# Attention scores from float16 halves of queries and keys at their own widths, and a half-width last key tile for the values

## The chip, the cores and the metric

One core of one Trainium2 chip runs the kernel. The metric is the device time of one execution in microseconds, the median over the runs. A core has five engines with an instruction stream each: TensorE (PE) multiplies matrices into PSUM, VectorE (DVE) and ScalarE (ACT) move and transform data, GpSimd (POOL) does element-wise work and SyncE (SP) issues most DMAs. ACT evaluates its functions from tables that an instruction of its own, ACT_TABLE_LOAD, exchanges.

## The reference

One step of a hybrid encoder layer on T = 1024 prompt rows and 32 sample rows of 1024 channels, 16 heads of 64. Both kinds of rows share the weights; the sample rows attend to 512 cached keys.

```python
h = rmsnorm(x, norm_g)
q = rmsnorm(h @ Wq, q_g) / 8;  k = rmsnorm(h @ Wk, k_g)      # per head
logf = log_sigmoid(h @ Wf + b_f);  c = cumsum(logf)
s = q @ k.T + c[query] - c[key], causal                        # float32
o = softmax(s) @ v
u = (h @ Wua) * sigmoid(h @ Wub);  conv = causal depthwise conv of width 31 over u
ya = (o * silu(ga)) @ w_pa;  yb = (silu(layernorm(conv)) * silu(gb)) @ w_pb
out = x + (sigmoid(ma) * ya + sigmoid(mb) * yb) @ w_out
```

k, v, logf and the end of u are outputs too. The gains q_g are about eight times as large as k_g in the inputs used.

## The kernel before

**Stages.** The rows stand as 1056 columns (prompt and sample), cut into three chunks of 352, and every float32 operand of a projection is held as two float16 halves, so that one projection is three float16 matmuls per tile (`pj` at L186, `x_split` at L556 for the input). The trace shows the stages at about these times: 0 to 72 us loading, normalising and splitting x with the first u projection; 72 to 205 the rest of u and the values' projection; 205 to 484 queries and keys, with the convolution's taps on DVE (L377); 484 to 570 the gates ga; 570 to 1042 attention, in which PE is filled with the other gates' projections between the attention blocks; 1042 to 1247 the last gates and the projections pa and pb; 1247 to the end the output projection.

**Queries and keys.** `qk` (L889) squares the projection's result, sums the squares of each head by matmuls with a block of ones (`sqh` on ACT, `sql` on POOL at L904, `pst` at L884 and L885), scales to `qn`, and splits `qn` into a high half `qh` (ACT, L929) and a low half `ql` (POOL, L930), both float32r (a float32 whose matmul PE does in one pass). They are written to DRAM as `s_q` and `s_k`. For keys, `qn` also goes out as an output (`kT`, L935) and its sample columns are copied to `ks_t` (L936). `forget_rows` (L846) makes the cumulative sums c of 16 heads on DVE and writes c as two float32r parts with rows of ones to `s_aq` and `s_ak`.

**Attention.** `Head.load` reads a head's halves back as four tiles: QB and KB of 128 rows (low and high halves crossed), QA and KA of 68 rows (high halves and the four rows of c). For each of 8 blocks of 128 queries, `scores` (L1139) does two float32r matmuls per up to 512 keys into `psS`: 128 keys more for each block, in one piece up to 512 and in two equal pieces above, and with at least 256 columns in each (`wm`). `top` subtracts the row's maximum (DVE), `soft` takes the exponential (ACT, L1166), `norm` divides (POOL, L1172), and `turn` transposes the probabilities on PE into `ptr` (L1186), from where ACT copies the first four tiles and DVE the others to `pt` (L1189). Once block 7 is turned, `values` (L1205) does 20 float32 matmuls of 256 query columns, key tile by key tile, on two halves of the array's columns in turn (even tiles j on one, odd ones on the other), into two `po` buffers, which ACT and DVE add into `ot`. For two blocks of queries that share a matmul, the last key tile reaches only the second one; the first one's half of `pt` is set to zero by POOL (L1179). `ptr`, `po` and some sums share one pool of two PSUM buffers, `psT`.

**Order.** Up to attention the order on PE, DVE and ACT is the program's; in attention PE, SP, DVE and ACT keep the program's order; POOL's order there, and after attention all but PE's, is set by a scheduler from the kernel's priorities and dependences. Between attention blocks, `layernorm` (L1239) puts in its pieces one at a time: of these, six pairs of Ln and Exp on ACT over 176 columns each (L1259, L1260) stand among the blocks of heads 8 to 10. After attention `mk_pa` (L1397) loads `sma` and takes a Tanh of it for each tile (L1401).

Of the kernel before, what the change touches and what calls it, by code (L numbers as in the profile page):

```python
# [29 lines left out]
CW = T + 30 + TS  # L30
LNO = ((0,), (1, 2), (3,), (4, 5), (6,), (7,), ())
# [22 lines left out]
def build(tc, xT, xt, wv, wf, ckT, cv, clT, stT, vec, cst, yT, kT, vO, lfO, cpT, csT):  # L54
# [8 lines left out]
    s_q = dram.tile([2, D, T], F32, name="s_q")  # L63
    s_k = dram.tile([2, D, T], F32, name="s_k")
    s_v = dram.tile([8, 128, D], F32, name="s_v")
    s_vs = dram.tile([TS, D], F32, name="s_vs")
    s_aq = dram.tile([H, 4, T], F32, name="s_aq")
    s_ak = dram.tile([H, 4, T], F32, name="s_ak")
# [15 lines left out]
    def f32(ap):  # L84
        return ap.bitcast(F32)
# [366 lines left out]
    with tc.high_priority(offset=9000):  # L452
# [15 lines left out]
        tops = xip.tile([128, 4], F32, name="tops0")  # L468
# [30 lines left out]
    qg8 = cp.tile([128, 1], F32, name="qg8")  # L499
    qs_t = cp.tile([128, 8, TS], F32, name="qs_t")  # L500
# [150 lines left out]

    def consts():
# [3 lines left out]
        nc.vector.tensor_scalar(qg8, vec_t[:, V_QG:V_QG + 1], 0.125, None, op0=ALU.mult)  # L656
# [6 lines left out]
    for f in range(8):  # L663
# [16 lines left out]
        1: [lambda: squares(3)],  # L680
        2: [lambda: low_pool(0, 2, True)],
# [4 lines left out]
        {2: [lambda: behind[0].pop(0)(), lambda: total(2), lambda: known(1)]})  # L686
# [159 lines left out]
    def forget_rows(lfT):  # L846
        on16 = fp.tile([H, T], F32R, name="on16")
        nc.gpsimd.memset(f32(on16), 1.0)
        ls = fp.tile([H, SKEYS], F32, name="ls")
        nc.sync.dma_start(ls[:, :PAST], clT)  # L850
        cc = fp.tile([H, T], F32, name="cc")
        csm = fp.tile([H, SKEYS], F32, name="csm")
        ch, cl, nch, ncl = [fp.tile([H, T], F32R, name=n) for n in ("ch", "cl", "nch", "ncl")]
        V = nc.vector
        ops = [
            (1.4, lambda: V.tensor_tensor_scan(cc, f32(on16), lfT[:, :T], 0.0, op0=ALU.mult, op1=ALU.add)),
            (0.1, lambda: V.tensor_copy(ls[:, PAST:], lfT[:, T:])),
            (0.8, lambda: (V.tensor_tensor_scan(csm, f32(on16)[:, :SKEYS], ls, 0.0, op0=ALU.mult, op1=ALU.add),
                           nc.sync.dma_start(s_cs, csm))),
            (0.8, lambda: V.tensor_copy(ch, cc)),  # L860
            (0.8, lambda: V.tensor_sub(cl, cc, f32(ch))),
            (0.8, lambda: V.tensor_scalar(nch, f32(ch), -1.0, None, op0=ALU.mult)),
            (0.8, lambda: V.tensor_scalar(ncl, f32(cl), -1.0, None, op0=ALU.mult)),
        ]

        def out():
            for dst, rows in ((s_aq, (on16, on16, ch, cl)), (s_ak, (nch, ncl, on16, on16))):
                for i, rw in enumerate(rows):
                    nc.sync.dma_start(dst[:, i, :], f32(rw))
# [19 lines left out]
    def qk(g, f):  # L889
        gv, dst, smp = (vec_t[:, V_KG:V_KG + 1], s_k, ks_t) if g == "k" else (qg8, s_q, qs_t)  # L890
# [33 lines left out]
        def out(c):  # L924
            n = CH if c < 2 else T - 2 * CH
            o = slice(c * CH, c * CH + n)
            qh = tp.tile([128, CH], F32R, name="qh", tag="qh")
            ql = tp.tile([128, CH], F32R, name="ql", tag="ql")
            nc.scalar.copy(qh[:, :n], qn[:, o])  # L929
            nc.gpsimd.tensor_sub(ql[:, :n], qn[:, o], f32(qh[:, :n]))  # L930
            nc.sync.dma_start(dst[0, f * 128:(f + 1) * 128, o], f32(qh[:, :n]))
            nc.sync.dma_start(dst[1, f * 128:(f + 1) * 128, o], f32(ql[:, :n]))
# [40 lines left out]
    class Head:  # L973
# [4 lines left out]
        def load(self):  # L978
            h = self.h
            self.q = [hp.tile([n, T], F32R, name=a, tag=a) for a, n in (("QA", 68), ("QB", 128), ("KA", 68),  # L980
# [3 lines left out]
            nc.sync.dma_start(f32(QB[0:64]), s_q[1, hs, :])  # L984
            nc.sync.dma_start(f32(QB[64:128]), s_q[0, hs, :])
            nc.sync.dma_start(f32(KB[0:64]), s_k[0, hs, :])
            nc.sync.dma_start(f32(KB[64:128]), s_k[1, hs, :])
            nc.sync.dma_start(f32(QA[0:64]), s_q[0, hs, :])
            nc.sync.dma_start(f32(QA[64:68]), s_aq[h])
            nc.sync.dma_start(f32(KA[0:64]), s_k[0, hs, :])  # L990
            nc.sync.dma_start(f32(KA[64:68]), s_ak[h])
# [141 lines left out]
    class Block:  # L1133
# [5 lines left out]
        def scores(self):  # L1139
# [7 lines left out]
            wm = max(w, 256)  # L1147
            for b in range(nb):
                ksl = slice(b * w, b * w + wm)
                nc.tensor.matmul(ps[:, b, :wm], QB[:, qsl], KB[:, ksl], start=True, stop=False)  # L1150
                nc.tensor.matmul(ps[:, b, :wm], QA[:, qsl], KA[:, ksl], start=False, stop=True)  # L1151
# [39 lines left out]
        def values(self):  # L1191
# [9 lines left out]
            for c in range(4):  # L1201
                po = pos[c // 2][:, 256 * (c % 2):256 * (c % 2) + 256]
                for j in range(2 * c + 2):
                    rows = slice(64 * (j % 2), 64 * (j % 2) + 64)
                    nc.tensor.matmul(po[rows], V[:, j, :], parts[c][:, j, :], start=(c % 2 == 0 and j < 2),  # L1205
# [500 lines left out]
```

## Time and profile before

| | |
|---|---|
| median of 3 runs | 1327.76 us (1327.39 to 1329.06) |
| span of the profiled execution | 1331.8 us |
| attention, 570 to 1042 | 472 us |
| DVE busy, whole span | 986.0 us |
| ACT busy, whole span | 693.1 us |
| POOL busy, whole span | 565.2 us |

The profiled execution is taken by the hardware profiler, and its span is 4.0 us above the median of the runs. Start and length of an instruction are in microseconds in the timeline, and nanoseconds stand as "mean ns" in the groups. A matmul's length is its latency: successive matmuls overlap, so what one costs PE is read from the distance of successive starts. LDWEIGHTS loads an operand into the array and overlaps with the matmul before. A wait in brackets says how long the engine sat idle and for what it waited.

### The profile page before, as it was taken

How to read it: one execution, taken by the hardware profiler on the slowest of the kernel's cores; microseconds unless marked ns; L12 is line 12 of the kernel's file. 1: busy time of each engine (PE TensorE's matmuls, PEld its weight loads, DVE VectorE, ACT ScalarE, POOL GpSimd, SP SyncE). 2: the span in 40 equal slices, each digit the busy share in tenths (PEclk: the TensorE clock that was granted, in tenths of full speed). 3: DMA queues.
4: the chain of work that ended last, by engine and by line, in shares of the span. 5: the costliest groups of instructions: out<-in, count | busy, mean ns of one | idle time of the engine just before them, and what ended most of it. 6: DMA issues, size and time to landing. Idle time of an engine off the chain costs nothing.

```text
span 1331.8 us, 24835 instructions
## 1 busy us (share of the span) xinstructions
PE 1311.1 (98%) x9396; PEld 1004.7 (75%) x9396; DVE 986.0 (74%) x1513; ACT 693.1 (52%) x1336; POOL 565.2 (42%) x597
## 2 busy tenths in 40 slices
PE   8999999999999999999899999999999999999999
PEld 5687876666666666677577767767777699999998
DVE  6797879889999998897787875754555388176664
ACT  5644545767686843455545555555555466233320
POOL 4001014637475730245445544342443258255562
PEclk8999999999999999999999999999999999999999
DMA  6243243425252553526545654465561788434461
GB/s 253 99 137 109 86 121 112 146 63 198 86 187 65 186 156 130 164 69 165 147 119 142 181 142 121 114 187 134 150 170 39 247 320 275 157 130 143 126 214 67
DMA packets 113495, 194.96 MB, mean 146 GB/s; under 512 B 34080, under 2 KB 80032, under 8 KB 113376
## 3 DMA queue, kind: packets, MB, share of 16 engines
q1 hardware_dynamic: 113232, 193.31, 46.9%
q8 instruction: 74, 1.21, 0.4%
q14 instruction: 45, 0.37, 0.1%
q10 hardware_dynamic: 144, 0.07, 0.0%
HBM read 127.68 MB, written 65.64 MB: 145 GB/s over the span
## 4 chain that ended last, share of the span: by engine, by line
PE 88%; DVE 7%; ACT 2%; issue 1%; DMA 1%; SPq 1%; POOL 0%; DVEq 0%; ACTq 0%; POOLq 0%
PE pj L186 59%; PE pjv L785 6%; PE pj L1537 6%; PE po L1205 5%; PE ptr L1186 4%; PE psS L1151 2%; PE psS L1150 2%; DVE y L377 2%; DVE wl L144 1%; DVE nm L1159 1%; DMA s_y<-y 1%; PE pst L884 1%; PE pst L885 0%; DMA ga<-s_ga 0%; PE ptx L586 0%
## 5 line engine op out<-in xcount | busy, mean ns | idle before, releaser
L186 PE MATMUL pj<-xl,wh 128*128 128x352 f16 (+2 forms) x1536 | 481.7, 314 | 1.8 <-DVE xl L593 1.6
L186 PE MATMUL pj<-xh,wh 128*128 128x352 f16 (+2 forms) x1536 | 482.2, 314 | 0.8 <-DVE qn L919 0.6
L186 PE MATMUL pj<-xh,wl 128*128 128x352 f16 (+2 forms) x1536 | 481.7, 314 | 0.0
L186 PEld LDWEIGHTS <-wh 128*128 128x128 f16 x3072 | 301.6, 98 | 161.7 <-issue 8.1
L377 DVE SCALAR_TENSOR_TENSOR y<-u,vec_t,y 128x1086 f32<-128x1086 f32 x240 | 348.5, 1453 | 12.1 <-ACT y L374 9.0
L1172 POOL TENSOR_SCALAR P<-P,nm 128x128 f32<-128x128 f32 (+7 forms) x128 | 140.9, 1101 | 203.3 <-DVE nm L1171 181.9
L186 PEld LDWEIGHTS <-wl 128*128 128x128 f16 x1536 | 150.8, 98 | 71.0 <-issue 1.4
L1166 ACT ACTIVATE P<-psS,nm 128x128 f32<-128x128 f32 (+7 forms) x128 | 95.1, 743 | 129.1 <-DVE nm L1171 111.8
L144 DVE SCALAR_TENSOR_TENSOR wl<-raw,sc,wh 128x384 f16<-128x384 f32 x188 | 133.3, 734 | 16.3 <-ACT wh L141 15.8
L1159 DVE TENSOR_REDUCE nm<-psS 128x1 f32<-128x128 f32 (+7 forms) x128 | 97.0, 758 | 10.7 <-POOL P L1172 0.5
L1186 PE MATMUL ptr<-ident,P 128*128 128x128 f32 x576 | 87.2, 274 | 9.8 <-DVE pt L1189 4.7
L1189 ACT COPY pt<-ptr 128x512 f32<-128x512 f32 (+3 forms) x128 | 64.4, 503 | 44.6 <-PE ptr L1186 44.3
L178 POOL TENSOR_TENSOR wl<-raw,wh 128x384 fp32r<-128x384 f32 (+1 forms) x51 | 60.9, 1221 | 61.8 <-ACT wh L175 46.7
L904 POOL TENSOR_TENSOR sql<-sqf,sqh 128x352 fp32r<-128x352 f32 x48 | 57.7, 1203 | 64.9 <-ACT sqh L901 64.9
L1186 PEld LDWEIGHTS ptr<-ident,P 128*128 128x128 f32 x576 | 69.0, 141 | 19.3 <-POOL rstd L357 3.7
L1150 PE MATMUL psS<-KB,QB 128*128 128x256 f32 (+2 forms) x192 | 81.6, 426 | 0.0
L120 POOL CAST topb<-tops 128x2 bf16<-128x2 f32 x35 | 18.6, 532 | 135.9 <-ACT junk L117 86.0
L1205 PE MATMUL po<-pt,V 128*64 128x256 f32 x640 | 72.6, 382 | 2.6 <-ACT pts L1107 2.6
L930 POOL TENSOR_TENSOR ql<-qn,qh 128x352 fp32r<-128x352 f32 (+1 forms) x48 | 67.6, 1424 | 6.1 <-ACT qh L929 6.0
L785 PE MATMUL pjv<-vwh,xh 128*128 128x260 f16 x256 | 70.1, 274 | 0.0
L785 PE MATMUL pjv<-vwl,xh 128*128 128x260 f16 x256 | 70.0, 273 | 0.0
L785 PE MATMUL pjv<-vwh,xl 128*128 128x260 f16 x256 | 69.9, 273 | 0.0
(277 smaller groups left out, 2572.1 us busy)
## 6 DMA issues: line engine op xcount, KB each, us to landing
raw<-wf SPq DMA_DIRECT2D x92, 512.0 KB
QB<-s_q SPq DMA_DIRECT2D x32, 256.0 KB
KB<-s_k SPq DMA_DIRECT2D x32, 256.0 KB
kT<-qn SPq DMA_DIRECT2D x8, 528.0 KB
s_ga<-t SPq DMA_DIRECT2D x24, 176.0 KB
s_gb<-t SPq DMA_DIRECT2D x24, 176.0 KB
s_ma<-t SPq DMA_DIRECT2D x24, 176.0 KB
s_mb<-t SPq DMA_DIRECT2D x24, 176.0 KB
```

The source lines that it names most:

```text
L144: nc.vector.scalar_tensor_tensor(wl[:, ks, :], raw[:, ks, :], self.s[:, i:i + 1], wh[:, ks, :], op0=ALU.mult, op1=ALU.subtract)
L186: nc.tensor.matmul(ps, a[:, kt, :], b(kt, sl), start=(first and n == 0), stop=(last and n == N - 1))
L377: t = nc.vector.scalar_tensor_tensor(y, u[:, i:i + CW], w, y, op0=ALU.mult, op1=ALU.add)
L785: nc.tensor.matmul(ps[:, :VC], a, b, start=(n == 0), stop=(n == 23))
L930: nc.gpsimd.tensor_sub(ql[:, :n], qn[:, o], f32(qh[:, :n]))
L1150: nc.tensor.matmul(ps[:, b, :wm], QB[:, qsl], KB[:, ksl], start=True, stop=False)
L1159: nc.vector.tensor_reduce(nm[:, 0:1], ps[:, :nb, :w], axis=AX.XY, op=ALU.max, negate=True)
L1166: nc.scalar.activation(P[:, :nk].rearrange("p (b w) -> p b w", b=nb), ps[:, :nb, :w], AF.Exp, bias=nm[:, 0:1], accum_out=nm[:, 1:2])
L1172: nc.gpsimd.tensor_scalar(P[:, :nk], P[:, :nk], nm[:, 2:3], 1.0, op0=ALU.mult, op1=ALU.mult)
L1186: nc.tensor.transpose(pt[:, 128 * j:128 * j + 128], P[:, 128 * (4 * u + j):128 * (4 * u + j) + 128], ident)
L1205: nc.tensor.matmul(po[rows], V[:, j, :], parts[c][:, j, :], start=(c % 2 == 0 and j < 2), stop=(c % 2 == 1 and j >= 2 * c))
L1537: nc.tensor.matmul(pss[c][:, :HC], a[:, k, :], x, start=(not more and kt == 0 and n == 0), stop=(kt == 3 and n == 2), skip_group_check=more)
```

## The change

1. Queries, keys and the sums are kept and read as float16: `s_q`, `s_k`, `s_aq`, `s_ak`, `qh`, `ql`, and the tiles QA, QB, KA and KB. The sums c are divided by 64 and written as three float16 parts beside rows of 64, so QA and KA have 70 rows. `forget_rows` has six DVE operations of 16 partitions for the four before.
2. The scores' matmuls have exactly the width of the keys; `wm` is gone, and block 0 has 128 columns.
3. Queries and keys are balanced by a power of two, worked out from the two gains by seven DVE operations of at most two columns and one matmul in the first chunk of `x_split` (`gains`, `balance`). Keys are therefore unscaled again for the output, by a new POOL operation `kun` over 128x1056.
4. In `values`, key tiles alternate between the halves of the array by j + c instead of j, and for c of 1 and more the last tile is multiplied over the second 128 columns alone. The memset of `pt` is left for c = 0.

```diff
-    s_q = dram.tile([2, D, T], F32, name="s_q")
+    s_q = dram.tile([2, D, T], F16, name="s_q")
...
+    def gains():
+        g = vec_t[:, V_QG:V_QG + 2]
+        nc.vector.tensor_mul(tops[:, 4:6], g, g)
+
+    def balance():
+
+        V = nc.vector
+        r = xip.tile([128, 2], F32, name="gr")
+        V.tensor_scalar(bits(r), bits(psq[:, 4:6]), 24, 23, op0=ALU.logical_shift_right, op1=ALU.logical_shift_left)
...
+        V.tensor_scalar(bits(bal[:, 1:2]), bits(r[:, 1:2]), -1.0, float(190 << 23), op0=ALU.mult, op1=ALU.add)
...
-        1: [lambda: squares(3)],
-        2: [lambda: low_pool(0, 2, True)],
+        1: [lambda: squares(3), gains],
+        2: [lambda: low_pool(0, 2, True), balance],
...
-        {2: [lambda: behind[0].pop(0)(), lambda: total(2), lambda: known(1)]})
+        {2: [lambda: behind[0].pop(0)(), lambda: total(2),
+             lambda: nc.tensor.matmul(psq[:, 4:6], ones_w, tops[:, 4:6], start=True, stop=True), lambda: known(1)]})
...
-            (0.8, lambda: V.tensor_copy(ch, cc)),
-            (0.8, lambda: V.tensor_sub(cl, cc, f32(ch))),
-            (0.8, lambda: V.tensor_scalar(nch, f32(ch), -1.0, None, op0=ALU.mult)),
-            (0.8, lambda: V.tensor_scalar(ncl, f32(cl), -1.0, None, op0=ALU.mult)),
+            (0.5, lambda: V.tensor_scalar(rc, cc, 1.0 / CU, None, op0=ALU.mult)),
+            (0.5, lambda: V.tensor_copy(cp3[:, 0, :], rc)),
+            (0.8, lambda: V.tensor_sub(rc, rc, cp3[:, 0, :])),
+            (0.5, lambda: V.tensor_copy(cp3[:, 1, :], rc)),
+            (0.8, lambda: V.tensor_sub(cp3[:, 2, :], rc, cp3[:, 1, :])),
+            (0.8, lambda: V.tensor_scalar(cn3, cp3, -1.0, None, op0=ALU.mult)),
...
             if c == 2:
                 if g == "k":
-                    nc.sync.dma_start(kT[f], qn)
-                nc.gpsimd.tensor_scalar(smp[:, f, :], qn[:, T:TT], 1.0, 1.0, op0=ALU.mult, op1=ALU.mult)
+                    kun = tp.tile([128, TT], F32, name="kun", tag="kun", bufs=1)
+                    nc.gpsimd.tensor_scalar(kun, qn, bal[:, 1:2], 1.0, op0=ALU.mult, op1=ALU.mult)
+                    nc.sync.dma_start(kT[f], kun)
+                    nc.gpsimd.tensor_scalar(smp[:, f, :], kun[:, T:TT], 1.0, 1.0, op0=ALU.mult, op1=ALU.mult)
+                else:
+                    nc.gpsimd.tensor_scalar(smp[:, f, :], qn[:, T:TT], bal[:, 0:1], 1.0, op0=ALU.mult, op1=ALU.mult)
...
-            wm = max(w, 256)
             for b in range(nb):
-                ksl = slice(b * w, b * w + wm)
-                nc.tensor.matmul(ps[:, b, :wm], QB[:, qsl], KB[:, ksl], start=True, stop=False)
-                nc.tensor.matmul(ps[:, b, :wm], QA[:, qsl], KA[:, ksl], start=False, stop=True)
+                ksl = slice(b * w, b * w + w)
+                nc.tensor.matmul(ps[:, b, :w], QB[:, qsl], KB[:, ksl], start=True, stop=False)
+                nc.tensor.matmul(ps[:, b, :w], QA[:, qsl], KA[:, ksl], start=False, stop=True)
...
-                nc.gpsimd.memset(self.head.p[c][:, i + 1, 0:128], 0.0)
+                if c == 0:
+                    nc.gpsimd.memset(self.head.p[c][:, 1, 0:128], 0.0)
...
-                    rows = slice(64 * (j % 2), 64 * (j % 2) + 64)
-                    nc.tensor.matmul(po[rows], V[:, j, :], parts[c][:, j, :], start=(c % 2 == 0 and j < 2),
+                    rows = slice(64 * ((j + c) % 2), 64 * ((j + c) % 2) + 64)
+                    n0 = 128 if c and j == 2 * c + 1 else 0
+                    nc.tensor.matmul(po[rows, n0:], V[:, j, :], parts[c][:, j, n0:], start=(c % 2 == 0 and j < 2),
```

The scheduler also moves work that the diff doesn't name. The first place is ACT's stream in attention, among the blocks of heads 8 to 10, where the layer norm's pairs stand; `t<-pj` empties a gate projection's PSUM, `pt<-ptr` empties the transposes, `P` is the softmax. Before:

```order
L968 ACTIVATE t<-pj,sc 128x352
L1189 COPY pt<-ptr_10056 128x4x128
L1166 ACTIVATE P,nm<-psS,nm 128x384
L117 ACTIVATE junk,tops<-raw 128x1024
L1259 ACTIVATE t<-rstd 128x176
L1260 ACTIVATE t<-t 128x176
L1189 COPY pt<-ptr_10098 128x128
```

The same place now, with the line numbers of the changed kernel (L1289 and L1290 are the pair, L997 the gate's copy, L1218 `pt`, L1194 the softmax):

```order
L997 ACTIVATE t<-pj,sc 128x352
L1289 ACT_TABLE_LOAD
L1289 ACTIVATE t<-rstd 128x176
L1290 ACT_TABLE_LOAD
L1290 ACTIVATE t<-t 128x176
L1218 COPY pt<-ptr_10055 128x4x128
L1194 ACTIVATE P,nm<-psS,nm 128x384
```

Each of the six pairs stands one piece later than before, between a gate's copy and a `pt` copy, and has two table loads, where before it had none. ACT's stream has 26 table loads for 14.

The second place is ACT's stream in attention some heads earlier, around the copies of a head's output `ot`. It reads now:

```order
L1194 ACTIVATE P,nm<-psS,nm 128x640
L1239 COPY ot<-po 64x512
L1431 ACT_TABLE_LOAD
L1431 ACTIVATE sma<-sma 128x352
L1239 COPY ot<-po 64x512
L1431 ACTIVATE sma<-sma 128x352
L1218 COPY pt<-ptr_9088 128x3x128
L1194 ACTIVATE P,nm<-psS,nm 128x768
```

In the kernel before, this table load and the first Tanh of `sma` (there L1401) stand after attention, at the start of pa. Now the first six of the 24 Tanh, and the loads of their tiles on SP, stand within attention, ahead of the six pairs.

The third place is POOL's stream in the queries' and keys' stage, at the end of a key projection. Before:

```order
L904 TENSOR_TENSOR sql<-sqf,sqh 128x352
L896 TENSOR_SCALAR gi<-sc,vec_t 128x1
L936 TENSOR_SCALAR ks_t<-qn 128x32
L904 TENSOR_TENSOR sql<-sqf,sqh 128x352
L930 TENSOR_TENSOR ql<-qn,qh 128x320
```

And now:

```order
L929 TENSOR_TENSOR sql<-sqf,sqh 128x352
L921 TENSOR_SCALAR gi<-sc,kgb 128x1
L961 TENSOR_SCALAR kun<-qn,bal 128x1056
L929 TENSOR_TENSOR sql<-sqf,sqh 128x352
L963 TENSOR_SCALAR ks_t<-kun 128x32
L955 TENSOR_TENSOR ql<-qn,qh 128x320
```

The new `kun` over 1056 columns stands ahead of a `sql`, where a copy of 32 columns stood.

Three smaller moves: head 0's loads of QA, QB, KA, KB and V stand some way earlier on SP; the write of the convolution's `s_y` stands behind later loads instead of ahead of them; DVE has the balance's operations between two `xl` of the first chunk. PE's order is the same, apart from a weight load of its own for each score matmul, the widths, and the one small matmul.

More of the change, by code (lines that the diff above doesn't have):

```diff
@@ L846, in forget_rows @@
     def forget_rows(lfT):
-        on16 = fp.tile([H, T], F32R, name="on16")
-        nc.gpsimd.memset(f32(on16), 1.0)
+        on16 = fp.tile([H, T], F32, name="on16")
+        nc.gpsimd.memset(on16, 1.0)
+        unit = fp.tile([H, T], F16, name="unit")
+        nc.gpsimd.memset(unit, CU)
         ls = fp.tile([H, SKEYS], F32, name="ls")
         nc.sync.dma_start(ls[:, :PAST], clT)
-        cc = fp.tile([H, T], F32, name="cc")
+        cc, rc = [fp.tile([H, T], F32, name=n) for n in ("cc", "rc")]
@@ L889, in qk @@
     def qk(g, f):
[L890 removed]
+        gv, dst, smp = (kgb, s_k, ks_t) if g == "k" else (qg8, s_q, qs_t)
         qn = tp.tile([128, TT], F32, name="qn", tag="qn")
```

59 lines of the change are left out of this document (34 added, 25 removed).

## Prediction

> **What bounds the kernel now.** I read the page's busy shares and chain first, then busy time by stage, then whom PE waits for in attention.
>
> ```profile
> PE 1311.1 (98%) x9396; PEld 1004.7 (75%) x9396; DVE 986.0 (74%) x1513; ACT 693.1 (52%) x1336; POOL 565.2 (42%) x597
> ...
> PE 88%; DVE 7%; ACT 2%; issue 1%; DMA 1%; SPq 1%; POOL 0%; DVEq 0%; ACTq 0%; POOLq 0%
> ```
>
> PE works for 1311 of 1331.8 us and is 88% of the chain that ended last. So a PE nanosecond saved is a nanosecond of the end, unless another engine is late there; and any new wait of PE is paid in full. The stages (columns: window, its length, then busy time by engine) tell where others are near:
>
> ```profile
> 635.00:705.00 70.00, 63.54 (x483) 45.31 (x482) 54.58 (x97) 34.94 (x78) 35.03 (x38) 0.98 0.48 127
> ...
> 1042.00:1247.00 205.00, 205.00 (x1300) 197.72 (x1298) 116.85 (x135) 89.90 (x119) 103.58 (x79) 1.00 0.60 208
> ```
>
> The stretch from 635 to 705 leaves PE idle for 6.5 of 70 us, more than any other of its length; after 1042 PE has no gap at all. In attention PE's longest waits are these (total, times, longest):
>
> ```profile
> PE ptr L1186 <- DVE pt L1189: 4.7, 3, 3.5
> PE po L1205 <- ACT pts L1107: 2.6, 2, 1.8
> PE ptr L1186 <- ACT pt L1189: 2.4, 2, 1.7
> ```
>
> They are waits for the copies that free the two `psT` buffers: PE runs in order, and a late `pt` copy stops the projection behind it too.
>
> **Scores.** A float16 projection matmul of 352 columns starts 150 ns after the one before, 0.425 ns a column. Float32r scores of 512, 320 and 256 columns are followed 0.235, 0.15 and 0.12 us later:
>
> ```profile
> 821.08 0.31 PE L186 MATMUL pj<-xh,wl 128*128 128x352 f16 x1
> 821.23 0.31 PE L186 MATMUL pj<-xl,wh 128*128 128x352 f16 x1
> ...
> 825.49 0.40 PE L1150 MATMUL psS<-KB,QB 128*128 128x512 f32 x1
> 825.73 0.40 PE L1151 MATMUL psS<-KA,QA 68*128 68x512 f32 x1
> 825.96 0.71 PE L1186 MATMUL ptr<-ident,P 128*128 128x128 f32 x5
> ...
> 840.50 0.31 PE L1151 MATMUL psS<-KA,QA 68*128 68x320 f32 x1
> 840.65 0.31 PE L1150 MATMUL psS<-KB,QB 128*128 128x320 f32 x1
> ...
> 856.83 0.28 PE L1151 MATMUL psS<-KA,QA 68*128 68x256 f32 x1
> 856.95 0.82 PE L1186 MATMUL ptr<-ident,P 128*128 128x128 f32 x6
> ```
>
> In float16 they would be 0.217, 0.136 and 0.109, so 18, 14 and 11 ns less. A head has six matmuls of 512 columns, six of 384, four of 448, four of 320 and two of 256; with 15 ns for 384 and 448, between their neighbours, that is 108 + 90 + 60 + 56 + 22 = 336 ns. Block 0's two matmuls go from 120 ns (256 columns) to 54 (128 columns): 132 ns. Together 0.47 us a head, 7.5 us for 16. The bound from the other side: each float16 score has a weight load of its own, and a load lasts 98 ns:
>
> ```profile
> L186 PEld LDWEIGHTS <-wh 128*128 128x128 f16 x3072 | 301.6, 98 | 161.7 <-issue 8.1
> ```
>
> If the 128-column matmuls are bound by it, block 0 saves 44 ns instead of 132, and the sum is 6.1 us. I take 7.5, since the projections load per matmul too and go at their columns' rate.
>
> **Values.** Twenty matmuls, recorded as 40, take 4.47 us a head (842.16 to 846.63), 0.22 us per matmul of one half of the array when the two halves work side by side, each half doing ten, in two parts:
>
> ```profile
> 842.16 4.54 PE L1205 MATMUL po<-pt,V 128*64 128x256 f32 x40
> 846.63 0.32 PE L186 MATMUL pj<-xh,wh 128*128 128x352 f16 x1
> ...
> 767.20 1.08 PE L1074 MATMUL psS<-kc,qs_t 64*32 64x512 f32 x8
> 768.08 0.26 PE L1075 MATMUL psS<-ks_t,qs_t 64*32 64x32 f32 x8
> ```
>
> So 20 part-slots of 0.22. Three of the twenty matmuls lose half their columns. Alternating by j + c spreads them, one half getting 18 slots and the other 19: one slot less, 0.22 us a head, 3.5 us in all, if the halves run on independently. If each pair waits for its slower member nothing is saved. The sample's rows speak for independence: four matmuls of 512 columns and four of 32 stand alternately in the program, each in two parts and each pair on a quarter of the array of its own. One by one the eight long parts would take 8 × 0.217 = 1.7 us; they take 1.08, and the short ones follow 0.88 after the first started, so the quarters ran side by side and ahead of the program's order. I take 3.5, with 0 for the other end. The Trainium skill, in "TensorE: Matmul & The Clock Gate", Part 3 (The mechanism), has it that matmuls start and end in program order without reordering; by that rule the last, halved tile would wait for its place and this term would be about 0.
>
> **Not realised.** Between 635 and 705 PE waits on DVE already. Two heads' savings there, 2 × 0.69 = 1.4, I count as lost to that wait (0 to 3).
>
> **Table loads.** The twelve new ones stand between a gate's copy and a `pt` copy, in six places. A load lasts 1.283 us, and nothing drains around it: the copy before ends at 1061.81, the load starts 1061.83, and the next function starts 1063.12, when it is through:
>
> ```profile
> 1061.26 0.55 ACT L968 ACTIVATE t<-pj,sc 128x352 f32<-128x352 f32 x1
> 1061.83 1.28 ACT L1401 ACT_TABLE_LOAD   x1
> 1063.12 1.66 ACT L1401 ACTIVATE sma<-sma 128x352 f32<-128x352 f32 x4
> ...
> L1260 ACT ACTIVATE t<-t 128x176 f32<-128x176 f32 x6 | 2.1, 350 | 0.2
> ...
> L1259 ACT ACTIVATE t<-rstd 128x176 f32<-128x176 f32 x6 | 2.0, 339 | 0.0
> ```
>
> So where a pair now comes, ACT spends 2 × 1.28 + 0.34 + 0.35 = 3.26 us. The first place, at 836:
>
> ```profile
> 835.70 0.55 ACT L968 ACTIVATE t<-pj,sc 128x352 f32<-128x352 f32 x1
> 836.14 0.58 ACT L1189 COPY pt<-ptr 128x512 f32<-128x512 f32 x1
> ...
> 838.46 0.27 PE L1186 MATMUL ptr<-ident,P 128*128 128x128 f32 x1
> ...
> 841.68 0.38 ACT L1189 COPY pt<-ptr 128x256 f32<-128x256 f32 x1
> ...
> 858.61 0.58 ACT L1189 COPY pt<-ptr 128x512 f32<-128x512 f32 x1
> ...
> 859.63 0.60 PE L1186 MATMUL ptr<-ident,P 128*128 128x128 f32 x4
> ...
> 836.00:873.00 37.00, 36.67 (x271) 26.58 (x271) 27.37 (x71) 21.38 (x54) 13.40 (x22) 1.00 0.57 137
> ```
>
> The copy moves from 836.14 to 839.4 and ends at 839.98. Its buffer is the one that the transpose at 838.46 writes, two tiles on, so PE waits 1.5 us. At the second place the copy at 841.68 ends at 845.3 instead of 842.06; it frees the buffer of the second `po`, which the values reach after six of their twenty matmuls, at 842.16 + 0.3 × 4.47 = 843.5: 1.8. At the fourth, the copy at 858.61 ends at 862.45, and the transposes at 859.63 need its buffer: 2.8. The same working at the third, fifth and sixth gives 0.2, 0.8 and 1.5, where more or less gate work stands between. The sum is 8.6. Bounds: within the stretch of 37 us ACT is busy 21.4, and with 12 × 1.28 = 15.4 more would be 36.8: just full, so if all its idle time could be used, nothing but about 2 us would be lost; with every load on PE's path it is 15.4. Each block's chain (scores, maximum, exponential, division, transposes) is fixed in PE's order and ACT waits for it within, so I take the middle, 8.6. The Trainium skill ("ScalarE: Activation LUTs", What ACT_TABLE_LOAD costs) puts a switch at 1283 ns and a drain of about 1380 more. The row above shows the first and not the second; with it the term would be about 25.
>
> The Tanh of `sma`, moved ahead, meets ACT waiting for `po` between the two `ot` copies: 0, and without that cover 1.3 + 6 × 0.5. Its loads pass SP's queue behind their own writes: 0. In 1042 to 1247 PE has no gap, so the work taken out there gives nothing.
>
> **The start.** Seven small DVE operations at 0.2 us each stand at 18 to 20 us, where PE waits for DVE:
>
> ```profile
> 7.90 0.16 DVE L516 SCALAR_TENSOR_TENSOR rs<-rs,n 128x2 f32<-128x2 f32 x1
> 8.10 0.16 DVE L517 SCALAR_TENSOR_TENSOR rs<-rs,n 128x2 f32<-128x2 f32 x1
> ...
> 18.96 0.27 PE L186 MATMUL pj<-xl,wh 128*128 128x256 f16 x1 [1.34 <-DVE xl L593]
> ```
>
> All on the path they cost 1.4, all in DVE's own gaps 0; I take 0.8.
>
> **Queries and keys.** `kun` takes between 1.1 and 1.4 us (bounds from POOL operations of this size, below), eight times, ahead of a `sql` that PE's `pst` waits for:
>
> ```profile
> L139 POOL TENSOR_SCALAR wh<-raw,sc 128x1024 f16<-128x1024 f32 x22 | 24.6, 1128 | 0.0
> ...
> L1172 POOL TENSOR_SCALAR P<-P,nm 128x1024 f32<-128x1024 f32 x16 | 22.7, 1417 | 15.3 <-DVE nm L1171 15.3
> ...
> 229.43 1.97 POOL L904 TENSOR_TENSOR sql<-sqf,sqh 128x352 fp32r<-128x352 f32 x1
> ...
> 233.71 0.32 PE L885 MATMUL pst<-sql,bones 128*128 128x352 f32 x1
> ```
>
> Here the `sql` ends at 231.4 and is needed at 233.7: 2.3 us cover 1.4. Beside DVE work POOL slows (this `sql` took 1.97), so I take 0.5, from 0 to 3. The two more operations of `forget_rows` lie in DVE's time beside projections that PE does meanwhile, the halved DMAs and the memsets that go were waited for by nothing on the path: 0 for each.
>
> **The sum.** -7.5 - 3.5 + 1.4 + 8.6 + 0.8 + 0.5 = +0.3 us: 1332.1 against the span of 1331.8, and since the median stands 4.0 below the profiled span, 1328.1. A measurement can tell 0.2%, 2.7 us, from no change.
>
> **Rivals.** *Loads hidden.* ACT absorbs the loads in its waits, as the window's 36.8 of 37 would allow: 2 instead of 8.6, 1321.5, and 1318 if the 3.5 us stall for DVE's `pt` goes too, as head 0's loads and the gate's come earlier. For it: PE has become faster before and after, ACT has 15 us of waits. Against: the copy that frees the buffer stands behind the loads. *ACT bounds.* The loads come wholly on PE's path, because each late exponential delays its block's transposes as well: 15.4 instead of 8.6, 1334.9; this decides once a pair's delay is longer than the block's distance of 3 us, and 3.26 is just over it. With the drain that the Trainium skill's page "ScalarE: Activation LUTs" (What ACT_TABLE_LOAD costs) adds, it would be about 1345 by the sum. *Pairs in step.* The values' halves don't run independently: 1331.6. *POOL late.* `kun` holds up `pst` by a mean 1 us each time: 8 instead of 0.5, 1335.6; it decides where the cover of `sql` is under 1.4 us, which at the place shown it isn't. That the change doesn't do what it says, the weight loads keeping scores where they are, would lose the 7.5: 1335.6, with little for it.
>
> **Chances.** The sum as it stands has 0.42, with 0.24 of it inside 0.2%, 0.08 below and 0.10 above. Loads hidden 0.28, faster. ACT bounds 0.12, slower. Pairs in step 0.10, of which 0.07 is slower and 0.03 the same. POOL late (or the scores unchanged) 0.08, of which 0.06 slower and 0.02 the same. So faster 0.36, same 0.29, slower 0.35. The range goes from 1318, the hidden loads with the stall gone, to 1337, over ACT bounds and POOL late; more than that (the drain, two mishaps at once) is left out.
>
> **What would show it.** In the profile after: score matmuls of 512 columns 0.217 us apart and block 0's 0.054; values in 4.25 us instead of 4.47; six waits of PE for ACT's `pt` of 0.2 to 2.8 us around 836 to 873, together 8.6; PE's waits at 18 to 21 longer by 0.8. If the values still take 4.47, the pairs are in step; if no wait for ACT appears, the loads are hidden; if `pst` waits for `sql`, POOL is late. The forecast is wrong if these six waits sum to less than 5 or more than 12 us.

## The result and the profile after

The changed kernel takes 1345.86 us (median of 4 runs, 1344.01 to 1347.72), the kernel before beside it 1327.70 (1327.39 to 1329.06). The ratio is 1.0132, with a 95% interval from 1.0116 to 1.0148: slower by about 18 us. The forecast was 1328.1, with a range from 1318 to 1337. The four runs of the changed kernel lie in two pairs, 1344.0 and 1344.1 with a mean granted clock of TensorE of 0.997 of full speed, and 1347.6 and 1347.7 with 0.995 and 0.993.

The profile of before that is shown above comes from an execution that was longer than most: its span is 1331.8 us, and a second profile of the same kernel has 1325.7, against 1342.3 for the changed kernel. The first has a halved TensorE clock from 20 to 27 us and a wait of 3.5 us near 647 us; the second has neither. So all comparisons below are with the second one. The page of before, second profile (span, busy time):

```profile
span 1325.7 us, 24835 instructions
...
PE 1306.7 (99%) x9396; PEld 1002.1 (76%) x9396; DVE 982.1 (74%) x1513; ACT 692.7 (52%) x1336; POOL 568.5 (43%) x597
```

And the changed kernel:

```profile
span 1342.3 us, 24807 instructions
...
PE 1303.8 (97%) x9398; PEld 977.5 (73%) x9398; DVE 978.6 (73%) x1523; ACT 708.5 (53%) x1348; POOL 579.1 (43%) x558
...
PE 81%; DVE 7%; DMA 3%; ACT 3%; issue 3%; POOL 2%; SPq 1%; DVEq 0%; POOLq 0%; ACTq 0%
```

PE is busy for 2.9 us less, and idle for 38.5 us (1342.3 - 1303.8) instead of 19.0. That is the loss: 19.5 - 2.9 = 16.6, the difference of the spans. ACT has 16 us more, about the twelve table loads. Whom PE waits for now, longest in total first (total, times, longest):

```profile
PE ptr L1215 <- ACT pt L1218: 8.8, 10, 2.6
PE pst L910 <- POOL sql L929: 5.0, 2, 4.5
PE po L1235 <- ACT pt L1218: 4.1, 2, 2.8
PE ptr L1215 <- DVE ot L1240: 3.0, 2, 2.0
PE ptr L1215 <- DVE os_t L1160: 2.7, 2, 1.4
PE po L1235 <- ACT pts L1136: 2.2, 2, 1.6
```

Second profile of before, the same view:

```profile
PE po L1205 <- ACT pts L1107: 2.6, 2, 1.8
PE ptr L1186 <- ACT pt L1189: 2.4, 2, 1.7
PE ptx L586 <- DVE xl L593: 1.8, 2, 1.3
PE ptr L1186 <- DVE pt L1189: 1.7, 2, 1.4
```

The largest waits that are new or grown are those for ACT's `pt` copies, for POOL's `sql`, and for DVE's `ot`. To see where the time goes, the starts of the same matmuls in the two profiles (timeline, us):

| matmul | before, second | after | later by |
|---|---|---|---|
| a projection after the first split | 13.48 | 14.26 | 0.8 |
| last `pst` of a key projection | 325.72 | 330.24 | 4.5 |
| projection behind it | 326.79 | 332.48 | 5.7 |
| last `pst` of a later one | 439.18 | 446.06 | 6.9 |
| values of head 5 | 743.2 | 750.2 | 7.0 |
| values of head 7 | 806.4 | 815.4 | 9.0 |
| second part of the values of head 9 | 864.60 | 884.14 | 19.5 |
| values of head 14 | 1005.23 | 1021.99 | 16.8 |

**The gains are there.** In heads without waits PE does each head faster. Scores of the changed kernel follow each other by their columns: 448 in 0.19 us.

```profile
950.01 0.35 PE L1178 MATMUL psS<-KB,QB 128*128 128x448 f16 x1
950.20 0.35 PE L1179 MATMUL psS<-KA,QA 70*128 70x448 f16 x1
950.40 0.35 PE L1178 MATMUL psS<-KB,QB 128*128 128x448 f16 x1
950.59 0.35 PE L1179 MATMUL psS<-KA,QA 70*128 70x448 f16 x1
950.78 0.60 PE L1215 MATMUL ptr<-ident,P 128*128 128x128 f32 x4
```

and the values last 4.32 us in the record instead of 4.54 (to the next matmul 4.26 instead of 4.47):

```profile
942.05 4.32 PE L1235 MATMUL po<-pt,V 128*64 128x256 f32 x40
```

From 923.52 to 1005.23 in before and 942.05 to 1021.99 after, three heads in which PE waits for nothing, the time falls from 81.71 to 79.94: 0.59 a head, which would be 9.4 over 16.

**The queries' and keys' stage.** POOL's stream in the changed kernel at the place where it loses 4.5 us (timeline):

```profile
321.29 2.17 POOL L961 TENSOR_SCALAR kun<-qn,bal 128x1056 f32<-128x1056 f32 x1 [3.21 <-DVE qn L944]
323.43 4.64 POOL L358 TENSOR_TENSOR rstd<-rstd,y 128x1024 f32<-128x1024 f32 x2
328.05 0.21 POOL L963 TENSOR_SCALAR ks_t<-kun 128x32 f32<-128x32 f32 x1
328.22 1.96 POOL L929 TENSOR_TENSOR sql<-sqf,sqh 128x352 fp32r<-128x352 f32 x1
```

The second profile of before at the same place:

```profile
318.76 3.79 POOL L357 TENSOR_TENSOR rstd<-rstd,y 128x1024 f32<-128x1024 f32 x2
323.04 0.22 POOL L936 TENSOR_SCALAR ks_t<-qn 128x32 f32<-128x32 f32 x1 [0.50 <-DVE qn L919]
323.22 0.93 POOL L904 TENSOR_TENSOR sql<-sqf,sqh 128x352 fp32r<-128x352 f32 x1
```

Before, the two sums of squares of the convolution (`rstd`) run while POOL waits for `qn`. Now `kun` stands ahead of them and waits 3.2 us for `qn` itself; then come 2.2 us of `kun`, 4.6 of `rstd` and 2.0 of `sql`, the last two longer than in before's rows (3.8 and 0.9), and `sql` is done at 330.2 instead of 324.1. What PE does:

```profile
330.24 0.66 PE L910 MATMUL pst<-sql,bones 128*128 128x352 f32 x1 [4.46 <-POOL sql L929]
...
331.01 0.50 PE L187 MATMUL pj<-xh,wl 128*128 128x352 f16 x1
331.30 0.50 PE L187 MATMUL pj<-xl,wh 128*128 128x352 f16 x1
...
333.55 0.31 PE L187 MATMUL pj<-xh,wl 128*128 128x352 f16 x1
333.70 0.31 PE L187 MATMUL pj<-xl,wh 128*128 128x352 f16 x1
```

After the wait nine matmuls follow each other by 0.29 us and not by 0.15, and only then does the old pace return. The windows show why (each row has the window, its length, the busy time of PE, PEld, DVE, ACT and POOL, then the granted clock, the DMA share and GB/s):

```profile
330.70:333.30 2.60, 2.60 (x10) 1.39 (x10) 1.25 (x2) 1.05 (x2) 1.74 (x4) 0.50 0.20 56
333.30:336.00 2.70, 2.70 (x19) 1.77 (x18) 1.95 (x2) 1.29 (x3) 2.14 (x3) 0.98 0.20 62
870.10:872.50 2.40, 2.40 (x10) 1.26 (x9) 1.77 (x5) 0.65 (x3) 0.66 (x1) 0.50 0.00 0
```

The clock is halved for about 2.5 us after the wait, here and once more at 870, after one of the waits below. Each time costs nine matmuls times 0.15, 1.3 us.

**The layer norm's pairs.** ACT at the first of the six (timeline):

```profile
838.18 0.55 ACT L997 ACTIVATE t<-pj,sc 128x352 f32<-128x352 f32 x1
838.74 1.28 ACT L1289 ACT_TABLE_LOAD   x1
840.04 0.35 ACT L1289 ACTIVATE t<-rstd 128x176 f32<-128x176 f32 x1
840.40 1.28 ACT L1290 ACT_TABLE_LOAD   x1
841.70 0.35 ACT L1290 ACTIVATE t<-t 128x176 f32<-128x176 f32 x1
841.95 0.57 ACT L1218 COPY pt<-ptr 128x512 f32<-128x512 f32 x1
```

A pair takes 3.3 us, with nothing lost around a load. PE's rows with a wait between 838 and 890 (the timeline, all else left out):

```profile
842.66 0.30 PE L1215 MATMUL ptr<-ident,P 128*128 128x128 f32 x1 [0.96 <-ACT pt L1218]
...
849.13 3.03 PE L1235 MATMUL po<-pt,V 128*64 128x256 f32 x28 [1.26 <-ACT pt L1218]
...
861.45 0.33 PE L1215 MATMUL ptr<-ident,P 128*128 128x128 f32 x1 [1.18 <-ACT pt L1218]
...
869.40 0.90 PE L1215 MATMUL ptr<-ident,P 128*128 128x128 f32 x3 [2.61 <-ACT pt L1218]
...
884.14 3.03 PE L1235 MATMUL po<-pt,V 128*64 128x256 f32 x28 [2.79 <-ACT pt L1218]
```

They sum to 8.8. (The first line of the list of waits above has 8.8 too, but that is another set: ten waits of transposes alone, some of them outside this stretch.)

**Ahead of that**, at 788, PE waits 2.0 us for DVE's `ot`, because DVE itself waits in its order for the write of the convolution's `s_y`, which reads `y` until 786.3:

```profile
786.28 1.33 DVE L344 TENSOR_TENSOR y<-y,shift 128x1024 f32<-128x1024 f32 x2 [4.36 <-DMA s_y<-y]
787.52 1.27 DVE L1240 TENSOR_TENSOR ot<-ot,po 64x512 f32<-64x512 f32 x2
```

That write is issued at 783.52, behind the loads of a head; in before it stood ahead of them.

### The profile page after: what moved, and what is told of

The parts are those of the page before. It is cut to its first block, busy times and chain, and to the rows that moved or that the text cites. A ratio compares the mean times of both kernels' runs of the same rounds, so it can differ in the third digit from the quotient of the medians.

```text
span 1342.3 us, 24807 instructions
## 1 busy us (share of the span) xinstructions
PE 1303.8 (97%) x9398; PEld 977.5 (73%) x9398; DVE 978.6 (73%) x1523; ACT 708.5 (53%) x1348; POOL 579.1 (43%) x558
## 4 chain that ended last, share of the span: by engine, by line
PE 81%; DVE 7%; DMA 3%; ACT 3%; issue 3%; POOL 2%; SPq 1%; DVEq 0%; POOLq 0%; ACTq 0%
PE pj L187 55%; PE pjv L805 6%; PE pj L1567 6%; PE po L1235 4%; PE ptr L1215 4%; DVE y L378 2%; PE psS L1179 2%; PE psS L1178 2%; DVE wl L145 1%; DVE nm L1187 1%; DMA raw<-wf 1%; POOL P L1200 1%; DMA xtok<-xt 1%; DMA s_y<-y 1%; PE pst L910 1%
## 5 line engine op out<-in xcount | busy, mean ns | idle before, releaser
L1200 POOL TENSOR_SCALAR P<-P,nm 128x128 f32<-128x128 f32 (+7 forms) x128 | 147.9, 1156 | 230.9 <-DVE nm L1199 202.5
L1194 ACT ACTIVATE P<-psS,nm 128x128 f32<-128x128 f32 (+7 forms) x128 | 95.1, 743 | 117.9 <-DVE nm L1199 109.9
L145 DVE SCALAR_TENSOR_TENSOR wl<-raw,sc,wh 128x384 f16<-128x384 f32 x188 | 123.3, 679 | 21.8 <-ACT wh L142 21.4
L179 POOL TENSOR_TENSOR wl<-raw,wh 128x384 fp32r<-128x384 f32 (+1 forms) x51 | 65.8, 1317 | 64.5 <-ACT wh L176 36.9
L1218 ACT COPY pt<-ptr 128x512 f32<-128x512 f32 (+3 forms) x128 | 64.3, 503 | 41.4 <-PE ptr L1215 40.9
L1235 PE MATMUL po<-pt,V 128*64 128x256 f32 (+1 forms) x640 | 69.6, 366 | 6.3 <-ACT pt L1218 4.1
L1235 PEld LDWEIGHTS po<-pt,V 128*64 128x64 f32 x640 | 45.0, 137 | 29.0 <-ACT pt L1218 5.4
L118 ACT ACTIVATE junk<-raw 128x1024 bf16<-128x1024 f32 x62 | 65.1, 1050 | 0.1
```

The lines of the kernel that those rows point to most:

```text
L118: nc.scalar.activation(junk[:, :raw.shape[1] * raw.shape[2]], raw.rearrange("p a b -> p (a b)"), AF.Square, accum_out=self.tops[:, i:i + 1])
L145: nc.vector.scalar_tensor_tensor(wl[:, ks, :], raw[:, ks, :], self.s[:, i:i + 1], wh[:, ks, :], op0=ALU.mult, op1=ALU.subtract)
L179: nc.gpsimd.tensor_sub(wl[:, k0:k1, :], raw[:, k0:k1, :], f32(wh[:, k0:k1, :]))
L1194: nc.scalar.activation(P[:, :nk].rearrange("p (b w) -> p b w", b=nb), ps[:, :nb, :w], AF.Exp, bias=nm[:, 0:1], accum_out=nm[:, 1:2])
L1200: nc.gpsimd.tensor_scalar(P[:, :nk], P[:, :nk], nm[:, 2:3], 1.0, op0=ALU.mult, op1=ALU.mult)
L1235: nc.tensor.matmul(po[rows, n0:], V[:, j, :], parts[c][:, j, n0:], start=(c % 2 == 0 and j < 2), stop=(c % 2 == 1 and j >= 2 * c))
```

## The experiments

Each was timed beside the kernel before on the same chip. Its median was 1329.73 in the first four, 1330.73 in the next four and 1329.06 in the last four, so ratios are given, and differences are taken between kernels that were timed together where that is possible. The changed kernel was timed apart from the twelve, so a difference to it can be off by 1 us or so: by the ratios the 12.1 and 6.6 below would be 13.3 and 7.6.

**A second profile of the kernel before**, unchanged.

> The kernel before once more, for a second profile of it. The profile on record has a span of 1331.8 us, 4 us above the median of its runs. Theory A, that this profile caught a longer execution (its TensorE clock was below full speed in the first 72 us): a span near 1326, so that the changed kernel's profile of 1342.3 is 16 us longer than it and not 10.5. Theory B, that profiling always adds about 4 us to this kernel: a span near 1332 again.

Span 1325.7 and 1327.44 us for this execution, 1328.4 as a median of 10. Theory A holds. The time of an execution is 1.8 us above its span, and the changed kernel's 1342.3 stands against 1325.7.

**The Tanh behind attention.**

```diff
...
-            nc.sync.dma_start(sma[c], s_g["ma"][f, :, csl(c)])
-            nc.scalar.activation(sma[c], sma[c], AF.Tanh, scale=0.5)
+            with tc.issue_after(sides["so"].ins):
+                nc.sync.dma_start(sma[c], s_g["ma"][f, :, csl(c)])
+            with tc.issue_after(sides["ot"].ins):
+                nc.scalar.activation(sma[c], sma[c], AF.Tanh, scale=0.5)
```

(`so` and `ot` are the last write and the last copy of attention.)

> The changed kernel with the first Tanh of sma and their loads kept behind attention, so that the twelve table loads in the layer norm's pairs are gone. Theory A, that the moved Tanh costs what TensorE lost between 835 and 884 us and at the Tanh's own places (10.5 and about 1 us in the two traces): 1334 us. Rival B, that a table load costs a drain besides its 1.28 us, or that other things move too: below 1330. Rival C, that the stalls there come from another place and only shift: above 1340.

1333.77 us, ratio 1.0032 (1.0019 to 1.0045): 12.1 less than the changed kernel. Theory A holds. Between 820 and 880 the wait for ACT is all but gone; the whole answer for that stretch:

```profile
PE ptr L1215 <- ACT pt L1218: 0.3, 1, 0.3
```

**No kun.**

```diff
-                    kun = tp.tile([128, TT], F32, name="kun", tag="kun", bufs=1)
-                    nc.gpsimd.tensor_scalar(kun, qn, bal[:, 1:2], 1.0, op0=ALU.mult, op1=ALU.mult)
-                    nc.sync.dma_start(kT[f], kun)
+                    nc.sync.dma_start(kT[f], qn)
...
```

> The changed kernel without the unscaling of the keys' output (kun): the scaled keys are written, so that part of the output is left out. GpSimd's order keeps the two sums of squares (rstd) ahead of the low half sql, as in the changed kernel. Theory A, that kun's own time ahead of sql makes TensorE wait: 5.5 us less, 1340. Rival B, that the order of rstd ahead of sql is the cause: about 1 to 2 us less, 1344, with a wait of pst for sql near 317 us still there.

1339.22 us, ratio 1.0075 (1.0057 to 1.0093): 6.6 less. The `pst` wait at that place is 1.3 us instead of 4.5, since `rstd` still stands ahead of `sql`, and the clock is not halved behind it. So theory A carries most, and the order that B names is the 1.3 that stay.

**Both.**

> The changed kernel without the early Tanh and without kun (the unscaling left out). If the two costs are separate they add up: 11.5 and 5.5 us less than 1345.9, 1329 us. If they share a cause, or if the changed kernel has other losses against the kernel before, more than 1332; if the gain of 11 us that was forecast for scores and values then shows, 1318 to 1320.

1327.14 us, ratio 0.9988 (0.9975 to 1.0000): 18.7 less by the medians, where 12.1 and 6.6 make 18.7 (by the ratios 1.4%, where 1.0 and 0.6 make 1.6). The two costs are separate and make up the whole 18. But the forecast gain of scores and values doesn't show: the kernel stands where before stands.

**kun on ScalarE**, with the Tanh behind attention; nothing is left out.

```diff
-                    nc.gpsimd.tensor_scalar(kun, qn, bal[:, 1:2], 1.0, op0=ALU.mult, op1=ALU.mult)
+                    nc.scalar.mul(kun, qn, bal[:, 1:2])
...
```

> The changed kernel with the first Tanh of sma kept behind attention and kun on ScalarE instead of GpSimd, nothing left out. Theory A, that kun cost through GpSimd's order (it stood ahead of rstd and sql): as without kun, 1327 us, with no wait of pst for sql above 1.5 us. Rival B, that unscaling 128x1056 eight times costs wherever it stands, since ScalarE's 1.1 us now come ahead of the casts that TensorE waits for: 1331 or more.

1326.88 us, ratio 0.9968 (0.9952 to 0.9984). Theory A holds: in the queries' and keys' stage a single wait of PE of 0.4 us is left, and none for `sql`. This is the change without its two losses. Its ratio says 0.3% faster than before, the profiles half of that: the spans are 1323.9 and 1325.7 (1324.1 for the kernel of the run "Both"), all three at a granted clock of 1.000.

**The planner's costs** (from the kernel with kun on ScalarE and the Tanh behind attention).

```diff
-            (0.8, lambda: V.tensor_sub(rc, rc, cp3[:, 0, :])),
-            (0.5, lambda: V.tensor_copy(cp3[:, 1, :], rc)),
-            (0.8, lambda: V.tensor_sub(cp3[:, 2, :], rc, cp3[:, 1, :])),
-            (0.8, lambda: V.tensor_scalar(cn3, cp3, -1.0, None, op0=ALU.mult)),
+            (0.6, lambda: V.tensor_sub(rc, rc, cp3[:, 0, :])),
+            (0.4, lambda: V.tensor_copy(cp3[:, 1, :], rc)),
+            (0.6, lambda: V.tensor_sub(cp3[:, 2, :], rc, cp3[:, 1, :])),
+            (0.6, lambda: V.tensor_scalar(cn3, cp3, -1.0, None, op0=ALU.mult)),
```

> The same with the planner's costs of the six operations of forget_rows set so that they sum to 3.2 as before (0.5, 0.5, 0.6, 0.4, 0.6, 0.6). Theory A, that these costs (3.9 in the changed kernel) put the convolution's taps one step later, so that the write of s_y falls behind a head's loads and VectorE waits for it: the wait near 780 us (1.7) and part of those near 645 and 792 go, 2 to 4 us less than with kun on ScalarE alone, 1324. Rival B, that the waits there come from TensorE being faster in attention: no change, 1327.

1326.64 us, ratio 0.9973 (0.9955 to 0.9991): no change. What A says of the write is so: with the costs as before, `s_y` is written ahead of the head's loads, and DVE's wait for it falls from 3.44 us

```profile
777.60 1.33 DVE L344 TENSOR_TENSOR y<-y,shift 128x1024 f32<-128x1024 f32 x2 [3.44 <-DMA s_y<-y]
```

to 0.30:

```profile
774.21 1.33 DVE L344 TENSOR_TENSOR y<-y,shift 128x1024 f32<-128x1024 f32 x2 [0.30 <-DMA s_y<-y]
```

But PE's waits between 570 and 835 sum to 11.6 us with it and 11.9 without. The wait was removed and others took its place, as B says.

**No alternation by c** (from the kernel without Tanh and kun).

```diff
-                    rows = slice(64 * ((j + c) % 2), 64 * ((j + c) % 2) + 64)
+                    rows = slice(64 * (j % 2), 64 * (j % 2) + 64)
```

> The changed kernel without the early Tanh and without kun (1327.1), with the last key tile still halved but the key tiles alternating by j as before, so that all halved tiles lie on one half of the array. Theory A, halves independent: the other half still does ten whole tiles, values take 4.47 us and not 4.26, 3.4 us more: 1330.5. Rival B, pairs in step in program order: the flip gains nothing, 1327.

1331.41 us, ratio 0.9999 (0.9980 to 1.0017). Timed beside it, the kernel with kun on ScalarE, which differs from this one in kun and in the alternation, took 1326.88, 4.5 less; and the values last 4.53 us in the record instead of 4.32. Theory A holds, the halves are independent. It also says that everything in the change but the values, freed of its two losses, is worth nothing at the end that this interval, 2.4 us to either side, can tell.

**The values alone**, in the kernel before.

> The kernel before with the change of values alone (alternation by j + c, last tile halved, 48 memsets gone). If the 0.21 us a head is all on TensorE's path: 3.4 us less than before. If part of it is hidden where VectorE bounds attention's first heads: 2.5. If nothing of it reaches the end: no change.

1325.41 us, ratio 0.9962 (0.9946 to 0.9978): 5 us less than the kernel before beside it, with an interval from 3 to 7 that holds the 3.4 and lies just above the 2.5. The profiles agree that it reaches the end: against the first one of before, which has the same wait of 3.5 us near 645, the values of head 0 start 2.2 us earlier, which is the slow clock at the start of that profile, and those of head 15 6.5.

**An Exp in place of the first six Tanh.**

```diff
-            nc.scalar.activation(sma[c], sma[c], AF.Tanh, scale=0.5)
+            nc.scalar.activation(sma[c], sma[c], AF.Exp if f < 2 else AF.Tanh, scale=0.5)
```

> The changed kernel with an Exp in place of the first six Tanh, so that these six stand where they stand now but need no other table, and the layer norm's pairs have no loads (the gate of those six tiles is computed wrongly, which changes no time). Theory A, that the twelve loads cost the five waits of TensorE for ScalarE's pt (8.8) and the slow clock behind the longest (1.6), and that the moved Tanh and its DMA cost the rest of the 12.1: 1345.9 - 10.4 = 1335.5. Rival B, that all 12.1 is the loads: 1333.8. Rival C, that most is the Tanh's wait for its DMA: 1340 or more.

1335.81 us, ratio 1.0057 (1.0040 to 1.0074): 10.1 less than the changed kernel. Theory A holds: the loads are 10 of the 12, and the Tanh with their DMA, at the places where they stand, the other 2. (The 2 is near what the times can tell; in the profiles, PE of the changed kernel falls 1.2 us behind that of "The Tanh behind attention" between 757 and 790 us, where these Tanh stand.)

**No balance** (from the kernel with kun on ScalarE).

```diff
-        1: [lambda: squares(3), gains],
+        1: [lambda: squares(3)],
...
-        V.tensor_scalar(bits(r), bits(psq[:, 4:6]), 24, 23, op0=ALU.logical_shift_right, op1=ALU.logical_shift_left)
...
-        V.tensor_scalar(bits(bal[:, 1:2]), bits(r[:, 1:2]), -1.0, float(190 << 23), op0=ALU.mult, op1=ALU.add)
+        nc.gpsimd.memset(bal, 1.0)
```

> The kernel with kun on ScalarE and no early Tanh (1326.9), without the seven operations and the matmul of the balance (the balance is set to 1). Theory A, that they cost 0.8 us at the start, as forecast and as the traces' offset at 14 us says: 1326.1 by the trace's offset, not to be told from noise by the time. Rival B, that their shift of the first projections costs more later: 2 us less or more.

1328.03 us, ratio 0.9990 (0.9979 to 1.0001), with runs from 1324.47 to 1328.16: the time tells nothing of 0.8 us. The positions in the profiles tell more: the same projection starts at 26.16 in before (second profile), 26.89 with kun on ScalarE and 26.13 without the balance, so the balance does cost some 0.7 us at the start, as A says.

**Short taps, before and with kun on ScalarE.** The same edit in both; the rest of the convolution is left out.

```diff
-            t = nc.vector.scalar_tensor_tensor(y, u[:, i:i + CW], w, y, op0=ALU.mult, op1=ALU.add)
+            n = 64 if f > 5 else CW
+            t = nc.vector.scalar_tensor_tensor(y[:, :n], u[:, i:i + n], w, y[:, :n], op0=ALU.mult, op1=ALU.add)
```

> The kernel before with the convolution's taps of the last two channel groups, most of which VectorE does in attention's first seven heads, over 64 columns instead of 1086 (the rest of the convolution is left out). It is the base for the next run. TensorE's waits of 635 to 705 us should go: 2 to 5 us less than before.

> The same shortening in the changed kernel with kun on ScalarE and no early Tanh. With full taps that one is 3 to 4 us faster than before, though the scores and values save 0.58 us a head, 9.3, in heads without waits. Theory A, that VectorE's load in the first eight heads takes the difference: with short taps the whole 9.3 less 0.8 for the start shows, 8.5 us less than the kernel before with short taps. Rival B, that the rest is lost elsewhere (softmax chain, ScalarE): again 3 to 4.

1320.72 us, ratio 0.9941 (0.9925 to 0.9958), and 1317.59, ratio 0.9917 (0.9902 to 0.9932). The base gains more than expected, 8.3 us. The difference between the two is 3.1 us, so theory A falls and B's number comes: freeing DVE of the taps does not release the scores' gain. PE's waits between 570 and 835 without the change, short taps, the whole answer:

```profile
PE ptr L1187 <- ACT pt L1190: 0.7, 1, 0.7
PE ptr L1187 <- DVE os_t L1132: 0.4, 1, 0.4
PE ptr L1187 <- DVE pt L1190: 0.2, 1, 0.2
```

and with it:

```profile
PE ptr L1216 <- ACT pt L1219: 1.8, 4, 0.8
PE ptr L1216 <- DVE os_t L1161: 1.4, 1, 1.4
PE ptr L1216 <- DVE ot L1241: 1.2, 2, 0.8
PE psS L1104 <- ACT P L1195: 0.6, 1, 0.6
```

Sums of 1.3 and 5.0: 3.7 us of new waits, for copies and sums on ACT and DVE, with no single one among them over 1.4. With full taps it is 7.4 in the second profile of before and 11.9 with kun on ScalarE: 4.5 us.

## Why the prediction was wrong

**What bounds the kernel**: right. PE's time and its waits are the whole difference.

**Scores, -7.5**: the mechanism was right, the size too large. Over the three heads without waits all of PE falls by 0.59 a head, of which 0.21 is the values; 0.38 is the scores, 6.0 over 16 heads. The sum had been made from rows rounded to 10 ns. In the trace's own nanoseconds the distance of two scores falls by 15 at 512 columns (233 to 218), 13 at 448, 12 at 384 and 320 and 9 at 256, and not by 18, 15, 15, 14 and 11. Block 0, 58 ns a matmul, was not bound by its weight load of 98. That 6.0 lies next to the 6.1 of the prediction's other bound is chance: that bound rested on the weight load.

**Values, -3.5**: right, 0.21 a head, and the halves do run on independently: without the alternation the time is 4.5 us longer. The rival of pairs in step fell. The records of the values from 942.05 show the order too: the halved last tile, the last one of the program, starts its second part 3.83 us after the first matmul, and the whole tile ahead of it in the program, on the other half, starts its second part at 3.94. What the Trainium skill says in "TensorE: Matmul & The Clock Gate", Part 3 (The mechanism), strict program order of matmuls, doesn't hold here across the two halves of the columns.

**Not realised, 1.4**: this step failed too, by some 5.5 us. It was too small, and for the wrong reason. It was put into the stretch from 635 to 705, where PE already waited. In fact PE's new waits between 570 and 835 are 4.5 us against a saving of nine or so heads of 0.59, 5 us: almost nothing of it reaches the end there. The new waits are for copies, sums and softmax on ACT, DVE and POOL. Why they grow when PE gets faster is argued and not shown: which step of the chain from the scores over the softmax to the `pt` copies sets them is open. Taking away one of its waits, and taking away most of DVE's taps, each left the sum of new waits about as it was.

**Table loads, 8.6**: right in mechanism, and in size partly by luck. The waits sum to 8.8, but place by place they are 1.0, 1.3, 1.2, 2.6, none and 2.8, where 1.5, 1.8, 0.2, 2.8, 0.8 and 1.5 were worked out. There is no drain. The Trainium skill's page "ScalarE: Activation LUTs" (What ACT_TABLE_LOAD costs) has one of 1380 ns for each switch; in this trace each function of the pairs starts 11 ns after the load ends. What was missing is the halved clock behind one of the waits, 1.3, which makes the loads 10. "The Tanh of `sma`, moved ahead: 0" failed by 1 to 2 us: the Exp in their place showed that.

**The start, 0.8**: right in size, and not at the place named. The waits near 19 and 21 us didn't grow (1.3 and 1.3 in before, 1.3 and 1.0 now). The new wait is that of the balance's matmul for the squared gains:

```profile
13.21 0.38 PE L706 MATMUL pj<-tops,ones_w 128*128 128x2 f32 x2 [1.09 <-DVE tops L657]
```

Of the 0.8 us behind it, 0.6 are left at 26 us; without the balance nothing is.

**Queries and keys, 0.5**: this is the step that failed in its mechanism. It was costed as `kun`'s own 1.1 to 1.4 us against the 2.3 us that cover `sql` at one place. But `kun` also waits for `qn`, and POOL is a queue: where `rstd` stood ahead of that wait, it now stands behind it, and the wait, `kun` (2.2 us here, and as a median of the eight, not 1.1 to 1.4), `rstd` and `sql` come one after the other. The cost was 4.5 us at one place out of eight, 0.5 to 1 at another, and 1.3 for the clock; without `kun` 6.6 us went. The row by which the cover was measured, near 230 us, has no `rstd`; the one at 320 has it. The sign that the prediction named for POOL being late, `pst` waiting for `sql`, is what the profile shows. That rival was named with 8 us, but with a chance of 0.08 and a point of decision that only counted `kun`'s length.

**Moves that were put at 0**: the later `s_y` write stalls DVE for 4.4 us and PE for 2.0, as the order had shown and the prediction didn't follow. Its removal alone gained nothing, though.

**The sum**: 0.3 was forecast, 18.2 measured. Of the 18 us between, 6 are POOL's queue, 3.5 the Tanh and the clock around the loads, and the rest, 7 to 8, is gain that was counted and didn't reach the end: with both losses removed the sum forecasts -8.8 (-7.5 - 3.5 + 1.4 + 0.8), and that kernel stood at 0.9988, 1.6 us below before, as the spans of the two profiles say too. (With kun on ScalarE it is 4.3 by the ratio and 1.8 by the spans.) Of these 7, 1.5 is the size of the scores, and most of the others are the 4.5 of new waits in attention's first nine heads, whose cause is open.

## What to carry to other kernels

An instruction put into an engine's queue costs not its own length alone but its wait, and moves everything behind that wait: list what stood between the old neighbours at every place where it recurs, not at one. Count a saving on the busiest engine only for stretches where nothing else is nearly late; elsewhere it comes back as many small waits, of which removing one changes nothing. And when a change frees time or buffers, look at what a scheduler pulls forward from the next stage: here a function of another table, by which untouched code a few heads later got twelve loads.

## What the runs showed of the hardware

A long wait of PE is paid more than once. A granted clock of 0.50, on record for 3.4 us that begin at most 0.8 us before or after the wait's end, came with waits of 2.6, 3.5, 4.4 and 4.5 us in the profiles of these runs, and with some of those of 1.8 us: with the planner's costs, with the Tanh behind attention, and with short taps and kun on ScalarE the clock fell at a wait of 1.83 us, in the changed kernel and others it didn't. Nor did it at waits of 2.0 (788 us) and 2.8 us (884 us) in the changed kernel, so the length of the wait alone doesn't decide. A dip slowed five to twelve projection matmuls from 0.15 to 0.29 us, which costs 0.7 to 1.7 us. The dips are part of why executions of one kernel differ: of the 6.1 us between the two profiles of before, some 2.6 are the slow clock at the start, 2.2 the wait at 647 us (3.5 for 1.4) and 1.4 the dip behind it.

Halves of the array that work on different output columns run ahead of the program's order: the values take 4.26 us with the halved tiles spread over both halves, and 4.46 with all of them on one. A change of table costs ACT 1.28 us in these traces, the load alone: all 26 loads of the changed kernel last 1283 ns, and behind the twelve in the pairs the function starts 11 ns after the load's end.
